# Left-side sums of the down product, begun one plain step earlier and in small tiles

## The chip, the cores and the metric

The kernel runs on one core of one Trainium2 chip. Five engines work side by side on that core: TensorE (PE in the profile, its weight loads PEld), VectorE (DVE), ScalarE (ACT), GpSimd (POOL) and SyncE (SP), which here only issues transfers. The metric is the device time of one execution in microseconds, taken as the median of three runs. The profile is of one further execution.

## The reference, cut to what matters

One decoder block on 256 tokens of width 2048, in float32: a half-step SwiGLU, a mixer (gated delta rule beside stick-breaking attention), a second half-step SwiGLU, a gated per-token embedding, and RMS norms between them. The change touches the two SwiGLU stages alone, whose inner width is 5632:

```python
def swiglu(x, w_gu, w_down):
    gate, up = jnp.split(x @ w_gu, 2, axis=-1)
    return (jax.nn.silu(gate) * up) @ w_down

h = h + 0.5 * swiglu(rms_norm(h, ffn1_norm[i]), ffn1_w_gu[i], ffn1_w_down[i])
...
h = h + 0.5 * swiglu(rms_norm(h, ffn2_norm[i]), ffn2_w_gu[i], ffn2_w_down[i])
```

## The kernel before, in words

**Numbers.** Every operand of a matmul is split into a high and a low part of the float32r type, and three matmuls (high by high, high by low, low by high) stand for one. The left side (activations, transposed) lies in `nTh`/`nTl` for the gate and up products and in `hTh`/`hTl` for the down product. One `hTh` tile holds one block of 512 inner columns as four slabs of 128 rows by 256 tokens. The weights stream in from memory: `weight_pair` (L67 to L79) loads 256 rows by 512 columns into `raw`, ScalarE casts them to `whi` (L77), VectorE subtracts to get `wlo` (L78). `whi` and `wlo` have three buffers each.

**Parts and groups.** `ffn` (L467) is called once for each SwiGLU, as "1" and "2". It walks over `PARTS` (L27): inner blocks 0 to 2, 3 to 6 and 7 to 10. Each part has one group "gu" for each of its inner blocks (gate and up, two 512-column products each for two halves of the tokens, four PSUM banks), and then two groups "dn" that multiply the part's `hTh`/`hTl` with the down weights, for output columns 0 to 1023 and 1024 to 2047. Of parts two and three, with four inner blocks each, the fourth "gu" group is called the part's last one here, and the third the one in front of it.

**Plain steps and sevenths.** In a group most rows are multiplied as they are: a plain step is 12 matmuls on one weight pair (L543 to L545), and after each `lanes.step()` (L546) lets every waiting generator go on to its next `yield`. The first `ns` row groups of 256 (`NS` = 4 for gate and up; `NS_DOWN` = 3 for down in parts two and three, 2 in part one) are instead multiplied in a seven-product scheme of 2 by 2 blocks. Its products ("sevenths", `Group.product`, L327) run inside the group before the one that they belong to: a gu group has 8 plain steps, numbered 0 to 7, and carries the seven products of its follower. `plan` (L392) puts them behind plain steps 1, 2, 3, 4, 5, 6, 7 when the follower is of the same kind, and behind 2, 3, 4, 5, 6, 7, 7 when it isn't. They run in the order of `SEVEN`: 0, 1, 2, 4, 3, 5, 6. The ones numbered 0, 4 and 6 take their left side straight from `hTh`/`hTl`, the others from sums.

**Right-side sums.** A seventh's weights come from four quarters that lie in tiles `R`. `halved` (L294) casts one to `shi` (ScalarE, L298) and subtracts to `slo` (VectorE, L299), two buffers each; `add` (L307) forms sums on VectorE, and `add_loaded` (L314) adds a quarter by a transfer of the GpSimd queue. `next_weights` (L85) writes these out ahead of the matmul that uses them: up to two further weight pairs, and one further seventh.

**Left-side sums.** `halves` (L423) makes them, in lane 1. For each two row groups it adds high and low part into a tile `S` (L455), forms four sums and differences in place (L461), casts to `Sh` (ScalarE, L463) and subtracts to `Sl` (VectorE, L464). `Sh` and `Sl` have one buffer each and are shared by the gu and the dn sums, so the dn ones can be written only when the last seventh that reads the gu ones (number 5) is done. `S` for two row groups is a tile with the tag `sil`, of one buffer, which also holds the activated gate from `gated` (L505) until `down_input` has transposed it (L485). `S` for one row group is a tile with the tag `nat`, of four buffers, which else holds the `part` copies of `product` (L349).

For the down product of parts two and three (`ns` = 3) there are thus one `S` of 1024 columns for row groups 0 and 1, and one of 512 for row group 2. The generator is added at the start of the part's last gu group (L524 to L525). It goes on behind plain step 0 (row groups 0 and 1) and, after one empty step, behind plain step 2 (row group 2).

**What sets the order.** The program is written out in this order, and a scheduler of the library then orders each engine's instructions: among those whose inputs and buffers it takes as free, the one written first. Each engine runs its own list strictly in that order on the chip. `tc.keep_in_program_order` ties an instruction behind the one written just before it on its engine. That is done for the first addition of row group 2 (L447 to L455), and for the casts and subtractions that write `hTh`/`hTl` at the end of the next group (L502, L503).

Of the kernel before, what the change touches and what calls it, by code (L numbers as in the profile page):

```python
# [10 lines left out]
F32 = mybir.dt.float32  # L11
F32R = mybir.dt.float32r
AF = mybir.ActivationFunctionType
ALU = mybir.AluOpType
# [12 lines left out]
PARTS = ((0, 3), (3, 7), (7, 11))  # L27
# [3 lines left out]
NS_DOWN = tuple(3 if i1 - i0 == 4 else 2 for i0, i1 in PARTS)  # L31


SEVEN = (0, 1, 2, 4, 3, 5, 6)
# [12 lines left out]
def block_kernel(ctx, tc, a, out):  # L47
    nc = tc.nc
# [14 lines left out]
    lanes = Lanes(4)  # L63
# [93 lines left out]
    def picker(hi, lo):  # L157
        return lambda k: (hi[k // 4][:, k % 4, :], lo[k // 4][:, k % 4, :])
# [68 lines left out]
    def block(j):  # L227
        return slice(j * NB, (j + 1) * NB)
# [191 lines left out]
    order += [("pair", a["w_pg"][2][g]) for g in range(KD // 2)] + [("pair", a["w_pp"][2])]  # L420
    order.append(("pair", a["w_pp"][3]))

    def halves(kind, his, los, ns, wait=0):  # L423


        for _ in range(wait):
            yield
        fp = current[0]

        sh = fp.tile([P, NS, 2, 2, P], F32R, tag="Sh", name="Sh")  # L430
        sl = fp.tile([P, NS, 2, 2, P], F32R, tag="Sl", name="Sl")

        def side(i, g):
            if i in (0, 4, 6):
                k, t = 2 * (g % 2) + (i > 0), i // 6
                c = slice(t * P, (t + 1) * P)
                return his[g // 2][:, k, c], los[g // 2][:, k, c]
            j, t = {1: (1, 1), 2: (0, 0), 3: (0, 1), 5: (1, 0)}[i]
            return sh[:, g, j, t, :], sl[:, g, j, t, :]

        sides[kind] = side

        for g0 in range(0, ns, 2):
            n = min(2, ns - g0)
            hi, lo = his[g0 // 2], los[g0 // 2]
            keep = lambda ins: ins
            if g0 and n == 1:  # L447

                keep = tc.keep_in_program_order
                yield  # L450
            if n == 2:
                x = fp.tile([P, 2 * NB], F32, tag="sil", name="S")
            else:
                x = act.tile([P, NB], F32, tag="nat", name="S", bufs=4)
            keep(nc.vector.tensor_tensor(out=x, in0=hi[:, 0:2 * n].bitcast(F32).rearrange("p k x -> p (k x)"),  # L455
                                         in1=lo[:, 0:2 * n].bitcast(F32).rearrange("p k x -> p (k x)"), op=ALU.add))
            xv = x.rearrange("p (g j t y) -> p g j t y", g=n, j=2, t=2)
            a11, a12, a21, a22 = (xv[:, :, j, t, :] for t in range(2) for j in range(2))
            for o, y, z, op in ((a22, a21, a22, ALU.subtract), (a21, a11, a21, ALU.subtract),
                                (a11, a22, a11, ALU.subtract), (a12, a11, a12, ALU.add)):  # L460
                nc.vector.tensor_tensor(out=o, in0=y, in1=z, op=op)  # L461
            sx = [y[:, g0:g0 + n].rearrange("p g j t y -> p (g j t y)") for y in (sh, sl)]
            nc.scalar.copy(sx[0], x)  # L463
            nc.vector.tensor_tensor(out=sx[1], in0=x, in1=sx[0], op=ALU.subtract)  # L464
            yield

    def ffn(n, nT, r, scale, next_norm, stat):  # L467
        xs = picker(*nT)
        late = callable(r)
        with tc.tile_pool(name="ffn", bufs=1) as fp:  # L470
            hTh, hTl = [], []
# [42 lines left out]
            for group, todo in ffn_plan[n]:  # L514
                if group.kind == "behind":
                    break
                dn = group.kind == "dn"
                i0 = PARTS[group.part][0]

                if dn and group.nb and not group.last:  # L520
                    lanes.add(1, halves("gu", *nT, NS))
                elif dn and group.nb and group.follower:
                    lanes.add(1, halves("behind", *nxt, NS_BEHIND, 4))
                elif not dn and group.follower.kind == "dn":  # L524
                    lanes.add(1, halves("dn", hTh[i0:], hTl[i0:], NS_DOWN[group.part]))  # L525
                if dn and group.last and nxt is None:
                    nxt = new_nT()
                if group.banks is None:
                    group.new_banks()
                for kind, one in todo:  # L530
                    if kind == "seventh":
                        group.follower.product(SEVEN[one])
                        continue
                    b, g = one
                    whi, wlo = next_weights()
                    for j in range(2):
                        k = 2 * g + j
                        xh, xl = picker(hTh, hTl)(2 * PARTS[group.part][0] * 2 + k) if dn else xs(k)
                        st, sp = not group.ns and k == 0, k == 2 * len(group.src[b]) - 1
                        for t in range(2):  # L540
                            c = slice(t * P, (t + 1) * P)
                            out = group.banks[2 * b + t]
                            nc.tensor.matmul(out, xh[:, c], whi[:, j, :], start=st, stop=False, skip_group_check=True)  # L543
                            nc.tensor.matmul(out, xh[:, c], wlo[:, j, :], start=False, stop=False, skip_group_check=True)  # L544
                            nc.tensor.matmul(out, xl[:, c], whi[:, j, :], start=False, stop=sp, skip_group_check=True)  # L545
                    lanes.step()  # L546
                    if g < len(group.src[b]) - 1:
                        continue
                    outs = group.banks[2 * b:2 * b + 2]
                    if dn:  # L550
                        nb = group.nb + b
                        for t in range(2):
                            hb = h[:, t, block(nb)]
                            nc.vector.scalar_tensor_tensor(out=hb, in0=outs[t], scalar=scale, in1=hb,
                                                           op0=ALU.mult, op1=ALU.add)
                            if group.last:
                                sumsq(stat, t, block(nb), nb)
                        if group.last:
                            norm_block(nxt, next_norm, nb, lambda: fp.tile([P, 2, 4, P], F32, tag="tT", name="tT"),
                                       mm_ps if group.follower or n == "2" else mx_ps)  # L560
                            lanes.advance(0)
                    elif b == 0:
                        if not late:
                            sil = gated(outs)
                    else:
                        if late:
                            r = r()
                            sil = gated(group.banks[0:2])
                            late = False
                        th = fp.tile([P, 4, T], F32R, tag="hTh", name="hTh", bufs=max(i1 - i0 for i0, i1 in PARTS))  # L570
                        tl = fp.tile([P, 4, T], F32R, tag="hTl", name="hTl", bufs=max(i1 - i0 for i0, i1 in PARTS))
                        hTh.append(th)
                        hTl.append(tl)
                        i0, i1 = PARTS[group.part]

                        last = (3 if i1 - i0 == 4 else 2) if len(hTh) == i1 else 0
                        gen = down_input(outs, sil, th, tl, last)
                        next(gen)

                        lanes.finish(0)  # L580
                        lanes.add(0, gen)
                        if last:
                            lanes.advance(0)
# [58 lines left out]
    with tc.tile_pool(name="fin", bufs=1) as fp:  # L642
# [34 lines left out]
        group, todo = ffn_plan["2"][-1]  # L677
        for _, (nb, g) in todo:
            whi, wlo = next_weights()
            for j in range(2):  # L680
                k = 2 * g + j
# [20 lines left out]
        for t in range(2):  # L702
            n = NB >> t
            for i in range(NB // n):
                gt = mm_ps("gt")[:, 0:n]
                products(gt, t, xs, ws, slice(i * n, (i + 1) * n))
                gated(e[t][:, i * n:(i + 1) * n], gt, slice(3 * NB + i * n, 3 * NB + (i + 1) * n), t, 3 + i)
            rt = rstd(stat, t)
            for j in range(4):
                c = slice(j * NB, (j + 1) * NB)  # L710

                if j == 0:
                    nc.scalar.activation(hf[:, t, c], hf[:, t, c], AF.Copy, scale=rt)
                else:
                    nc.vector.tensor_scalar(out=hf[:, t, c], in0=hf[:, t, c], scalar1=rt, scalar2=None, op0=ALU.mult)
                queue = nc.sync if j % 2 else nc.scalar
                queue.dma_start(out=out[t * P:(t + 1) * P, c], in_=hf[:, t, c])


class Lanes:  # L720


    def __init__(self, n):
        self.q = [[] for _ in range(n)]
# [656 lines left out]
```

## Time and profile before

| what | value |
|---|---|
| runs | 1947.93, 1948.83, 1949.49 us |
| median | 1948.83 us |
| the profiled execution's own time | 1948.68 us |
| its span, first to last instruction | 1947.0 us |
| granted TensorE clock, mean | 0.999 |
| ACT busy | 1163.5 us (60%) |
| POOL busy | 148.4 us (8%) |

The profiled execution lies 0.15 us below the median of the three runs, and 1.7 us of its time lie outside its span. Times in the profile count from the start of the span. The matmuls are pipelined: one lasts some 0.39 us by its record, and the next begins before it ends, so that PE can read as busy where it lost time. The start-to-start distance of matmuls is the better measure, and the part below uses it. The four places that the change touches are the last gu group of parts two and three in both SwiGLU stages; they begin near 340, 588, 1485 and 1733 us.

### The profile page before, as it was taken

The numbers are of one execution on the slowest core, as the hardware profiler recorded it, in microseconds if no ns is written. First come the engines' busy times: TensorE is split into PE (matmuls) and PEld (weight loads), VectorE is DVE, ScalarE is ACT, GpSimd is POOL, SyncE is SP. The second block draws the span as 40 slices with busy tenths as digits, with TensorE's granted clock in tenths as the row PEclk, the third lists the DMA queues.
The fourth block names the chain that finished last, engine by engine and source line by source line (L and its number), as shares of the span: only waits on it lengthen the run. The fifth ranks groups of instructions, "written<-read, shape, count | busy, mean of one in ns | idle before, by whom it ended". The sixth has DMA issues, their size and how long they took to land.

```text
span 1947.0 us, 24130 instructions
## 1 busy us (share of the span) xinstructions
PE 1930.5 (99%) x8884; PEld 1593.0 (82%) x8884; DVE 1569.3 (81%) x1679; ACT 1163.5 (60%) x1358; POOL 148.4 (8%) x226
## 2 busy tenths in 40 slices
PE   9999999999999999999999999999999999999998
PEld 8888888888888888878788888888888888888886
DVE  7889878997889766797856579899888987888865
ACT  7656666566565557664555456566565755656654
POOL 0011100000010000010100000010000100001000
PEclk9999999999999999999999999999999999999999
DMA  8778888788887765556565786788898987888764
GB/s 314 267 238 282 254 296 273 229 294 250 279 284 240 225 219 170 176 171 208 171 204 160 242 290 227 225 291 283 243 281 249 314 260 240 272 255 293 232 213 144
DMA packets 144182, 475.04 MB, mean 244 GB/s; under 512 B 19649, under 2 KB 47297, under 8 KB 129857
## 3 DMA queue, kind: packets, MB, share of 16 engines
q1 hardware_dynamic: 107200, 302.16, 43.9%
q0 software_dynamic: 25920, 160.44, 30.2%
q10 hardware_dynamic: 10944, 10.91, 1.8%
q8 instruction: 69, 1.13, 0.2%
q14 instruction: 49, 0.39, 0.1%
HBM read 451.44 MB, written 22.02 MB: 243 GB/s over the span
## 4 chain that ended last, share of the span: by engine, by line
PE 88%; DVE 7%; DMA 3%; ACT 1%; issue 1%; POOL 0%; SPq 0%; POOLq 0%; DVEq 0%; ACTq 0%
PE d L545 5%; PE d L543 5%; PE d L544 5%; PE g L343 4%; PE g L344 4%; PE g L342 4%; PE u L544 4%; PE u L545 4%; PE u L543 4%; PE g L544 4%; PE g L545 4%; PE pj L112 4%; PE pj L113 4%; PE pj L114 4%; PE g L543 4%; PE d L343 2%
## 5 line engine op out<-in xcount | busy, mean ns | idle before, releaser
L77 ACT CAST whi<-raw 128x1024 fp32r<-128x1024 f32 (+1 forms) x489 | 512.1, 1050 | 422.7 <-PE pj L114 99.0
L78 DVE TENSOR_TENSOR wlo<-raw,whi 128x1024 fp32r<-128x1024 f32 (+1 forms) x489 | 592.3, 1218 | 162.3 <-ACT whi L77 161.2
L299 DVE TENSOR_TENSOR slo<-R,shi 128x2048 fp32r<-128x2048 f32 (+2 forms) x224 | 444.9, 1989 | 140.0 <-ACT shi L298 138.2
L298 ACT CAST shi<-R 128x2048 fp32r<-128x2048 f32 (+2 forms) x224 | 373.5, 1671 | 128.5 <-DVE R L307 62.7
L112 PE MATMUL pj<-whi,nTh 128*128 128x512 f32 x448 | 179.4, 401 | 0.0
L113 PE MATMUL pj<-wlo,nTh 128*128 128x512 f32 x448 | 175.2, 391 | 1.1 <-DVE wlo L78 1.1
L114 PE MATMUL pj<-whi,nTl 128*128 128x512 f32 x448 | 174.9, 390 | 0.0
L543 PE MATMUL d<-whi,hTh 128*128 128x512 f32 x448 | 174.5, 390 | 0.0
L544 PE MATMUL d<-wlo,hTh 128*128 128x512 f32 x448 | 174.3, 389 | 0.0
L545 PE MATMUL d<-whi,hTl 128*128 128x512 f32 x448 | 173.4, 389 | 0.0
L544 PE MATMUL g<-wlo,nTh 128*128 128x512 f32 x400 | 156.0, 390 | 0.5 <-DVE wlo L78 0.5
L544 PE MATMUL u<-wlo,nTh 128*128 128x512 f32 x400 | 155.7, 389 | 0.4 <-DVE wlo L78 0.4
L545 PE MATMUL g<-whi,nTl 128*128 128x512 f32 x400 | 155.8, 389 | 0.0
L545 PE MATMUL u<-whi,nTl 128*128 128x512 f32 x400 | 155.7, 389 | 0.0
L543 PE MATMUL g<-whi,nTh 128*128 128x512 f32 x400 | 155.3, 390 | 0.0
L543 PE MATMUL u<-whi,nTh 128*128 128x512 f32 x400 | 154.1, 389 | 0.0
L307 DVE TENSOR_TENSOR R<-R 128x2048 f32<-128x2048 f32 (+2 forms) x68 | 135.8, 1996 | 0.1
L113 PEld LDWEIGHTS pj<-wlo,nTh 128*128 128x128 f32 x448 | 84.2, 188 | 18.9 <-DVE wlo L78 2.6
L543 PEld LDWEIGHTS d<-whi,hTh 128*128 128x128 f32 x448 | 84.1, 188 | 18.2 <-ACT hTh L502 1.0
L545 PEld LDWEIGHTS d<-whi,hTl 128*128 128x128 f32 x448 | 84.1, 188 | 17.8
L114 PEld LDWEIGHTS pj<-whi,nTl 128*128 128x128 f32 x448 | 84.1, 188 | 17.5
L544 PEld LDWEIGHTS d<-wlo,hTh 128*128 128x128 f32 x448 | 84.1, 188 | 17.4
(332 smaller groups left out, 3444.1 us busy)
## 6 DMA issues: line engine op xcount, KB each, us to landing
raw<-in_w_gu SPq DMA_DIRECT2D x199, 512.0 KB, 5.7
raw<-in_w_down SPq DMA_DIRECT2D x112, 512.0 KB, 6.9
raw<-in_w_in SPq DMA_DIRECT2D x112, 512.0 KB, 3.4
R<-in_w_gu2q POOLq DMA_DIRECT2D x54, 1024.0 KB, 8.6
R<-in_w_gu1q POOLq DMA_DIRECT2D x48, 1024.0 KB, 8.6
raw<-in_w_out SPq DMA_DIRECT2D x32, 512.0 KB, 4.5
tT<-scr SPq DMA_DIRECT2D x22, 512.0 KB, 5.0
R<-in_w_down11q POOLq DMA_DIRECT2D x12, 768.0 KB, 6.2
```

What stands on the lines that cost most here:

```text
L77: nc.scalar.copy(hi[:, j, :], raw[:, j, :])
L78: nc.vector.tensor_tensor(out=lo[:, j, :], in0=raw[:, j, :], in1=hi[:, j, :], op=ALU.subtract)
L112: nc.tensor.matmul(outs[t], xh[:, c], whi[:, j, :], start=st, stop=False)
L113: nc.tensor.matmul(outs[t], xh[:, c], wlo[:, j, :], start=False, stop=False)
L114: nc.tensor.matmul(outs[t], xl[:, c], whi[:, j, :], start=False, stop=sp)
L298: keep(nc.scalar.copy(hi, w))
L299: nc.vector.tensor_tensor(out=lo, in0=w, in1=hi, op=ALU.subtract)
L307: keep(nc.vector.tensor_tensor(out=self.raw[x], in0=self.raw[x], in1=self.raw[y], op=ALU.add))
L343: nc.tensor.matmul(out, xh, wlo[:, g, :], start=False, stop=False, skip_group_check=True)
L543: nc.tensor.matmul(out, xh[:, c], whi[:, j, :], start=st, stop=False, skip_group_check=True)
L544: nc.tensor.matmul(out, xh[:, c], wlo[:, j, :], start=False, stop=False, skip_group_check=True)
L545: nc.tensor.matmul(out, xl[:, c], whi[:, j, :], start=False, stop=sp, skip_group_check=True)
```

## The change

For parts two and three the generator of the down sums is no longer added at the start of the part's last gu group. It is added in the group in front of it, right behind seventh number 5 of that group's follower, the last that reads the gu sums. It goes on first behind plain step 7 of that group, then twice in the last group, behind plain steps 0 (empty) and 1. So each of its pieces is written one plain step sooner. It also goes through the row groups one at a time (`at_once` = 1): three `S` tiles of 512 columns, all of the tag `nat`, in place of one of 1024 of the tag `sil` and one of 512. Row groups 0 and 1 are still written in one go, and row group 2 keeps its tie to the instruction written before it. `Later` looks the `hTh` tiles up when they are used, since the last ones don't exist yet when the generator is made. Part one, the gu sums and the ones called "behind" stay as they are.

```diff
-    def halves(kind, his, los, ns, wait=0):
+    def halves(kind, his, los, ns, wait=0, at_once=2):
...
-        for g0 in range(0, ns, 2):
-            n = min(2, ns - g0)
-            hi, lo = his[g0 // 2], los[g0 // 2]
+        for g0 in range(0, ns, at_once):
+            n = min(at_once, ns - g0)
+            k0 = 2 * (g0 % 2)
+            hi, lo = (x[g0 // 2][:, k0:k0 + 2 * n] for x in (his, los))
             keep = lambda ins: ins
-            if g0 and n == 1:
+            if g0 == 2 and n == 1:
...
-            yield
+            if not g0 % 2 + n == 1 or g0 + n == ns:
+                yield
...
-                elif not dn and group.follower.kind == "dn":
+                elif not dn and group.follower.kind == "dn" and not group.part:
                     lanes.add(1, halves("dn", hTh[i0:], hTl[i0:], NS_DOWN[group.part]))
...
                     if kind == "seventh":
-                        group.follower.product(SEVEN[one])
+                        follower = group.follower
+                        follower.product(SEVEN[one])
+                        if group.part and not dn and one == 5 and follower.kind == "gu" and \
+                                follower.follower.kind == "dn":
+                            p = PARTS[group.part][0]
+                            lanes.add(1, halves("dn", Later(hTh, p), Later(hTl, p), NS_DOWN[group.part], 0, 1))
                         continue
...
+class Later:
+
+
+    def __init__(self, blocks, first):
+        self.blocks, self.first = blocks, first
+
+    def __getitem__(self, i):
+        return self.blocks[self.first + i]
```

More of the change, by code (lines that the diff above doesn't have):

```diff
@@ L454, in halves @@
                 x = act.tile([P, NB], F32, tag="nat", name="S", bufs=4)
-            keep(nc.vector.tensor_tensor(out=x, in0=hi[:, 0:2 * n].bitcast(F32).rearrange("p k x -> p (k x)"),
-                                         in1=lo[:, 0:2 * n].bitcast(F32).rearrange("p k x -> p (k x)"), op=ALU.add))
+            keep(nc.vector.tensor_tensor(out=x, in0=hi.bitcast(F32).rearrange("p k x -> p (k x)"),
+                                         in1=lo.bitcast(F32).rearrange("p k x -> p (k x)"), op=ALU.add))
             xv = x.rearrange("p (g j t y) -> p g j t y", g=n, j=2, t=2)
```

## The prediction

> **What bounds the kernel now.** I read the page first, then the busy time by stretches, and last the timelines of single engines round the four places of the change.
>
> ```profile
> span 1947.0 us, 24130 instructions
> ...
> PE 1930.5 (99%) x8884; PEld 1593.0 (82%) x8884; DVE 1569.3 (81%) x1679; ACT 1163.5 (60%) x1358; POOL 148.4 (8%) x226
> ```
>
> PE is busy 99% of the span and the matmuls aren't changed, so the most that can be won is the time in which PE starts its matmuls late. A stretch without trouble and the four places of the change, by stretches of 48 us (columns: us, then for each engine busy us and instructions):
>
> ```profile
> 230.00:278.00 48.00, 48.00 (x214) 39.73 (x213) 37.32 (x26) 29.20 (x26) 4.84 (x7) 1.00 0.86 267
> ...
> 340.00:388.00 48.00, 47.64 (x209) 38.41 (x208) 43.24 (x46) 27.96 (x30) 4.84 (x7) 1.00 0.77 227
> 588.00:636.00 48.00, 47.64 (x208) 38.41 (x207) 43.23 (x45) 28.27 (x30) 4.84 (x7) 1.00 0.77 227
> 1485.00:1533.00 48.00, 47.64 (x208) 38.43 (x207) 43.23 (x45) 28.36 (x30) 4.80 (x7) 1.00 0.77 229
> 1733.00:1781.00 48.00, 47.64 (x208) 38.43 (x207) 43.23 (x45) 28.69 (x30) 4.79 (x7) 1.00 0.78 227
> ```
>
> The reader is to see the second column: 214 matmuls in the clean stretch, 208 or 209 in the others. The granted clock (1.00) is the same, so 5 or 6 matmuls' time is lost at each place. The four rows are alike, so I work out the first and multiply by four. Its PE timeline has the size:
>
> ```profile
> 340.08 0.39 PE L543 MATMUL g<-whi,nTh 128*128 128x512 f32 x1
> ...
> 348.01 0.39 PE L545 MATMUL g<-whi,nTl 128*128 128x512 f32 x1
> 348.24 0.39 PE L342 MATMUL d<-shi,hTh 128*128 128x512 f32 x1
> ...
> 362.98 0.50 PE L342 MATMUL d<-shi,Sh 128*128 128x512 f32 x1
> 363.32 0.40 PE L343 MATMUL d<-slo,Sh 128*128 128x512 f32 x1
> ...
> 368.20 0.40 PE L545 MATMUL u<-whi,nTl 128*128 128x512 f32 x1
> 368.73 0.50 PE L343 MATMUL d<-slo,hTh 128*128 128x512 f32 x1
> 369.07 0.40 PE L344 MATMUL d<-shi,hTl 128*128 128x512 f32 x1
> ...
> 376.57 0.39 PE L342 MATMUL d<-shi,hTh 128*128 128x512 f32 x1
> 377.18 0.50 PE L343 MATMUL d<-slo,hTh 128*128 128x512 f32 x1 [0.22 <-DVE slo L299]
> 377.52 0.40 PE L344 MATMUL d<-shi,hTl 128*128 128x512 f32 x1
> ```
>
> From 340.08 to 348.01 lie the 36 matmuls of three plain steps, 35 distances: 7.93 / 35 = 0.227 us each. The five long distances are 0.34, 0.53, 0.34, 0.61 and 0.34 us, together 2.16; less 5 x 0.227 = 1.13 they lose **1.03 us**. Smaller ones of some 0.01 us between them add the rest: by the counts, (214 - 209) x 0.227 = 1.1 to (214 - 208) x 0.227 = 1.4 us. I take 1.03 as the sure part and 1.2 as all of it, so 4.1 to 4.8 us for the four places.
>
> Why PE waits there is in the timelines of DVE and then of ACT for the same place, and in the busy time of the three stretches before, in and behind the crowd (third engine column: DVE):
>
> ```profile
> 301.71 1.28 DVE L503 TENSOR_TENSOR hTl<-tT,hTh 128x512 fp32r<-128x512 f32 x2
> ...
> 336.36 1.76 DVE L299 TENSOR_TENSOR slo<-R,shi 128x1536 fp32r<-128x1536 f32 x1 [1.10 <-ACT shi L298]
> ...
> 343.35 1.30 DVE L485 STREAM_TRANSPOSE tb<-sil 128x512 f32<-128x512 f32 x2
> ...
> 345.68 1.22 DVE L455 TENSOR_TENSOR S<-hTh,hTl 128x1024 f32<-128x1024 f32 x1
> ...
> 351.74 1.22 DVE L78 TENSOR_TENSOR wlo<-raw,whi 128x1024 fp32r<-128x1024 f32 x1
> ...
> 354.09 0.69 DVE L455 TENSOR_TENSOR S<-hTh,hTl 128x512 f32<-128x512 f32 x1
> 354.84 1.76 DVE L299 TENSOR_TENSOR slo<-R,shi 128x1536 fp32r<-128x1536 f32 x1
> ...
> 363.59 0.68 DVE L464 TENSOR_TENSOR Sl<-S,Sh 128x512 fp32r<-128x512 f32 x1
> 366.92 1.76 DVE L299 TENSOR_TENSOR slo<-R,shi 128x1536 fp32r<-128x1536 f32 x1 [2.65 <-ACT shi L298]
> ```
> ```profile
> 333.07 1.14 ACT L502 CAST hTh<-tT 128x512 fp32r<-128x512 f32 x2
> 334.84 1.49 ACT L298 CAST shi<-R 128x1536 fp32r<-128x1536 f32 x1 [0.63 <-PE u L344]
> ...
> 365.40 1.48 ACT L298 CAST shi<-R 128x1536 fp32r<-128x1536 f32 x1
> ```
> ```profile
> 303.00:336.40 33.40, 33.40 (x149) 27.67 (x148) 27.46 (x20) 22.28 (x22) 3.07 (x5) 1.00 0.94 278
> 336.40:360.80 24.40, 24.40 (x109) 20.19 (x109) 24.26 (x28) 11.49 (x12) 1.77 (x2) 1.00 0.73 205
> 360.80:382.00 21.20, 20.84 (x90) 16.25 (x89) 16.57 (x18) 14.31 (x15) 2.19 (x4) 1.00 0.83 294
> ```
>
> DVE is full from 336.4 to 360.8 (24.26 of 24.40 us), has 5.9 us to spare in the 33.4 us before, and 4.6 us to spare right after, where PE then waits for DVE. So the trouble is order. Row group 2 starts at 354.09 and its `Sl` ends at 364.27, ten microseconds for six short DVE instructions and one cast, as other work lies between them. Sevenths 1 and 2 can't end before that, so both `shi`/`slo` buffers stay taken, the next `shi` cast waits until 365.40 and the next `slo` until 366.92. From there the subtractions follow each other too closely, and PE catches up with one at 368.20 and with another at 376.57.
>
> **The change part by part.** First the durations, from the rows of the tile `S` in that place (min/median/max ns; the smaller is the short form):
>
> ```profile
> L461 DVE TENSOR_TENSOR S<-S x8: 282/353/424, 348.5 to 360.5; 128x256 f32<-128x256 f32 x4, 128x128 f32<-128x128 f32 x4
> L455 DVE TENSOR_TENSOR S<-hTh,hTl x2: 687/952/1218, 345.7 to 354.1; 128x1024 f32<-128x1024 f32 x1, 128x512 f32<-128x512 f32 x1
> L463 ACT CAST Sh<-S x2: 619/838/1057, 351.9 to 362.3; 128x1024 fp32r<-128x1024 f32 x1, 128x512 fp32r<-128x512 f32 x1
> L464 DVE TENSOR_TENSOR Sl<-S,Sh x2: 684/954/1225, 352.9 to 363.6; 128x1024 fp32r<-128x1024 f32 x1, 128x512 fp32r<-128x512 f32 x1
> ```
>
> *Tiles.* Row groups 0 and 1 cost now 1.22 + 4 x 0.42 + 1.23 = 4.1 us on DVE and 1.06 on ACT. As two small tiles they cost 2 x (0.69 + 4 x 0.28 + 0.68) = 5.0 us on DVE and 1.24 on ACT: **0.9 us more DVE** and 0.2 us more ACT at each place. Hidden, it costs nothing; with DVE full and nothing given back, 4 x 0.9 = 3.5 us.
>
> [...]
>
> *Start.* Now the large `S` waits for its `sil` buffer until the transposes have read it (343.35 + 1.30), so it could not begin sooner however early it was written; it begins at 345.68. A `nat` buffer is free long before. That sums of this kind run ahead of the place where they are written shows the next pair of rows: the gu sums of the following group begin at 391.30, while the evictions of the group in front, written before them, run at 412.95 and later.
>
> ```profile
> 391.30 1.23 DVE L455 TENSOR_TENSOR S<-nTh,nTl 128x1024 f32<-128x1024 f32 x1
> ...
> 412.95 1.28 DVE L554 SCALAR_TENSOR_TENSOR h<-d,h 128x512 f32<-128x512 f32 x2
> ```
>
> Row groups 0 and 1 read only the part's first block, whose last piece is finished at 302.99 (301.71 + 1.28). So I expect their additions, 2 x (0.69 + 4 x 0.28) = 3.6 us, in the 5.9 us to spare between 303 and 336.4, at no cost. Their `Sh` and `Sl` must wait for seventh 5 of the gu group, as `Sh` is shared; PE ends it near 334.8, since the `shi` cast of 334.84 waits for the same seventh. They then fall into the DVE hole of 1.10 us that ends at 336.36.
>
> *The crowd.* The DVE work between 336.4 and 360.8 loses 4.1 us and gets at most 1.4 us (two `Sl`) back. Of it, 2.9 us (1.22 + 4 x 0.42) lie ahead of the `wlo` of 351.74. Row group 2 moves from behind that `wlo` to ahead of it, 0.69 + 4 x 0.28 = 1.8 us. It so starts some 5 us sooner, near 349, and ends by about 354 in place of 364.27, as seventh 1 needs it (PE reaches it 9 + 12 matmuls behind 348.24, at 348.24 + 21 x 0.227 = 353.0). The `slo` that now runs at 366.92 then follows seventh 1 as soon as its buffer is free, near 356: the 4.6 us that DVE has to spare behind 360.8 are used before it. Of PE's waits 0.53 and 0.61 us, with the 0.34 us behind each and the 0.34 at 362.98, none has a cause left.
>
> *Moved past.* ACT's casts of `hTh` for the block in front are tied behind the new `Sh` casts. Behind them wait the next `shi` and `whi`, and DVE's `hTl`: with two small casts (1.24 us) and the two of `hTh` (1.14 us) ahead of it, the `shi` of 334.84 slips by up to 2.4 us, and its `slo` from 336.36 to 338.8, done at 340.5. The seventh that needs them starts at 348.24, so over 7 us cover it. If that cover were gone, 2.4 us would show at each place. SP and POOL get no new transfer; POOL's adding transfers wait only on R and its readers. The extra `nat` tiles hold three of four buffers at most, while the `part` copies use one at a time. I find nothing in these rows that is late next, but a first use of a fresh operand costs 0.34 - 0.227 = 0.1 us, as the three distances of 0.34 show, and one may stay.
>
> *Sum.* Four places x 1.05 us (between the sure 1.03 and 1.2 less 0.1) = **4.2 us**. The profiled execution's 1948.68 would become 1944.5; it lies 0.15 us below the median of the runs shown, so I predict 1948.83 - 4.2 = **1944.6 us**. All of it gone is 1944.0.
>
> **The rivals.**
>
> *Half of it.* The wait at 368.20 goes, but the order that the scheduler now finds leaves the one at 376.57, or makes a like one, as the list of each engine is fixed and PE's lead over `slo` is small there. For it: this second wait comes eight microseconds after the first, with other sevenths. Against: it is the same backlog. That leaves some 0.6 us of 1.2, so 4 x 0.55 = 2.2 us gained: 1946.6 us.
>
> *It doesn't do what it says.* Row group 2, which ends last, is still drawn out by the work between its instructions. Then sevenths 1 and 2 end as late as now: 1948.8 us.
>
> *The crowd moves forward (slower).* If the small tiles of row groups 0 and 1 do not run ahead, they are done where they are written, from 335.3 on: 5.0 us, less the hole of 1.10, push everything by 3.9 us. The `wlo` of 351.74 then comes at 351.74 + 3.9 - 2.9 + 1.8 = 354.5 and ends at 355.8, while PE first uses it at 353.90:
>
> ```profile
> 353.90 0.39 PE L544 MATMUL u<-wlo,nTh 128*128 128x512 f32 x1
> ```
>
> PE would wait 1.9 us and lose 0.1 more at the next start: 2.0 us at each place. It decides from the point where that `wlo` ends over 0.94 us later than now (351.74 + 1.22 = 352.96). With the old waits gone the net is +0.8 x 4 (1952.1 us), with all of them still there +2.0 x 4 (1956.8); I take the middle, 1954.4 us. Against it is the row of 391.30.
>
> *Only the price is paid.* DVE stays the limit through the whole crowd, nothing is gained, and the 0.9 us show: + 3.5 us, 1952.3 us. [...] Against it: DVE has 5.9 us free before and 4.6 us behind.
>
> **How the numbers follow.** Full effect 0.52, half 0.27, no effect 0.08, crowd forward 0.09, only the price 0.04. A measurement of this kernel can tell about 0.2% from no change, that is 3.9 us. The full effect reaches from 3.4 to 4.8 us; I give 0.46 to more than 3.9 and 0.06 to less. Faster is then 0.46. Within 0.2% lie 0.06 + 0.27 + 0.08, the price's 0.04 and 0.02 of the crowd: 0.47. Slower is 0.07. The range has to hold the full and the half effect (0.79): from 1944.0, less 0.5 for the spread of the runs, 1943.5, up to 1948.3, half a microsecond short of no effect, since the waits that remain in the half case may be 1.1 us each. The likeliest case's own range is 1943.5 to 1945.6.
>
> **What would show it.** Right: matmul counts of 212 to 214 in the four stretches; no distance over 0.3 us between the sevenths of the down group; `S` of row groups 0 and 1 before 336 us, and the `Sl` of row group 2 by about 355; DVE with nothing left idle at 361 to 367. Wrong: `S` of 512 columns only from 335 on, with a wait on `wlo` near 354 (crowd forward); `Sl` of row group 2 after 360 (no effect); a `slo` wait of 0.3 us or more near 376 (half). The prediction is wrong as a whole if the scheduler's new order costs PE time away from these four places, which I haven't priced because no row of the trace points to a place.

## The result and the profile after

The changed kernel takes **1958.34 us** (median of six runs, 1958.13 to 1959.99) against 1948.91 us for the kernel before (six runs, 1947.93 to 1949.49). The ratio is 1.0051, with an interval of 1.004 to 1.0061: some 9.4 us slower, where 4.2 us less were predicted. The profiled execution took 1958.19 us.

First the page of the changed kernel, span and busy times:

```profile
span 1956.5 us, 24152 instructions
...
PE 1933.3 (99%) x8884; PEld 1594.1 (81%) x8884; DVE 1573.7 (80%) x1703; ACT 1163.2 (59%) x1362; POOL 148.4 (8%) x226
```

The work on the engines is nearly what it was: DVE has 4.4 us more over the whole kernel (1573.7 less 1569.3). That isn't the price of the small tiles: the kernel below that has them at the old place keeps DVE busy for 1569.9 us. PE has the same 8884 matmuls. So the loss is again in late starts. Here are the busy times of the clean stretch and of the four places, by the same stretches as before (us, then for each engine busy us and instructions; then the granted clock):

```profile
230.00:278.00 48.00, 48.00 (x214) 39.74 (x213) 37.15 (x26) 29.18 (x25) 4.85 (x7) 1.00 0.87 267
340.00:388.00 48.00, 45.54 (x198) 36.44 (x197) 41.94 (x43) 27.40 (x31) 4.84 (x7) 1.00 0.75 225
588.00:636.00 48.00, 46.21 (x201) 37.20 (x200) 42.46 (x51) 27.16 (x31) 4.19 (x7) 1.00 0.74 239
1485.00:1533.00 48.00, 45.28 (x190) 36.14 (x189) 41.30 (x51) 27.06 (x30) 3.96 (x7) 0.96 0.75 238
1733.00:1781.00 48.00, 46.93 (x204) 37.84 (x203) 43.20 (x51) 28.88 (x32) 4.44 (x7) 1.00 0.79 257
```

The reader is to see the matmuls: 198, 201, 190 and 204 in place of 209, 208, 208 and 208. That is 11 + 7 + 18 + 4 = 40 fewer, and 40 x 0.227 us = 9.1 us, nearly all of the 9.5 us between the two profiled executions. The clean stretch has its 214 as before. The old five distances at each place gave way to longer ones, as the PE timeline at the first place shows:

```profile
349.14 0.39 PE L342 MATMUL d<-shi,hTh 128*128 128x512 f32 x1
...
358.66 0.39 PE L342 MATMUL d<-shi,Sh 128*128 128x512 f32 x1
359.42 0.74 PE L550 MATMUL u<-whi,nTh 128*128 128x512 f32 x2 [0.38 <-ACT whi L77]
360.27 0.51 PE L343 MATMUL d<-slo,Sh 128*128 128x512 f32 x1
360.62 0.40 PE L344 MATMUL d<-shi,Sl 128*128 128x512 f32 x1
...
375.83 0.39 PE L344 MATMUL d<-shi,Sl 128*128 128x512 f32 x1
376.89 0.50 PE L342 MATMUL d<-shi,hTh 128*128 128x512 f32 x1 [0.68 <-ACT shi L298]
378.69 0.50 PE L343 MATMUL d<-slo,hTh 128*128 128x512 f32 x1 [1.29 <-DVE slo L299]
379.03 0.40 PE L344 MATMUL d<-shi,hTl 128*128 128x512 f32 x1
```

The first row is for comparison. This matmul, the first of the sevenths for the down group, starts at 349.14 here and at 348.24 in the kernel before. The same 0.9 us lies between the two ahead of all that the change moves (DVE's last subtraction of a `part` copy before it, 330.92 and 330.02), so 0.9 us of any difference in time between these two traces is no effect of the change.

There are two groups of waits: from 358.66 to 360.62 lie four distances (two matmuls share the row of 359.42), 1.96 - 4 x 0.227 = 1.05 us lost, waiting for a weight cast `whi` and a `slo`; from 375.83 to 379.03 three distances, 3.20 - 0.68 = 2.5 us lost, waiting for `shi` and `slo`. The next two views show what DVE and then ACT did (the changed lines shift the numbers by one or two: the sums' additions are L456 and L462, `Sh` L464, `Sl` L465). The `slo` for which PE waits at 360.27 is the one of 358.46:

```profile
336.07 1.29 DVE L456 TENSOR_TENSOR S<-hTh,hTl 128x512 f32<-128x512 f32 x2
337.27 1.70 DVE L462 TENSOR_TENSOR S<-S 128x128 f32<-128x128 f32 x8
...
340.06 1.29 DVE L465 TENSOR_TENSOR Sl<-S,Sh 128x512 fp32r<-128x512 f32 x2 [0.42 <-ACT Sh L464]
...
344.26 1.76 DVE L299 TENSOR_TENSOR slo<-R,shi 128x1536 fp32r<-128x1536 f32 x1
...
351.59 1.22 DVE L78 TENSOR_TENSOR wlo<-raw,whi 128x1024 fp32r<-128x1024 f32 x1
352.72 1.75 DVE L307 TENSOR_TENSOR R<-R 128x1536 f32<-128x1536 f32 x1
354.39 0.69 DVE L456 TENSOR_TENSOR S<-hTh,hTl 128x512 f32<-128x512 f32 x1
...
358.46 1.76 DVE L299 TENSOR_TENSOR slo<-R,shi 128x1536 fp32r<-128x1536 f32 x1 [0.69 <-ACT shi L298]
```
```profile
356.42 0.62 ACT L464 CAST Sh<-S 128x512 fp32r<-128x512 f32 x1 [4.48 <-DVE S L462]
356.95 1.48 ACT L298 CAST shi<-R 128x1536 fp32r<-128x1536 f32 x1
358.32 1.04 ACT L77 CAST whi<-raw 128x1024 fp32r<-128x1024 f32 x1
...
372.90 1.05 ACT L77 CAST whi<-raw 128x1024 fp32r<-128x1024 f32 x1 [4.38 <-DMA raw<-in_w_down]
```

Row groups 0 and 1 were added at 336.07 and not in the spare time before 336. Row group 2 began at 354.39 in place of 354.09; counted from PE's first seventh that is 0.6 us sooner and not five. And ACT stood idle for 4.48 us, until 356.42, in front of row group 2's `Sh` cast, with a `shi` and a `whi` behind it in its list. In the kernel before the same `shi` and `whi` stood ahead of that cast, which came at 362.31 there:

```profile
353.33 1.48 ACT L298 CAST shi<-R 128x1536 fp32r<-128x1536 f32 x1
354.71 1.05 ACT L77 CAST whi<-raw 128x1024 fp32r<-128x1024 f32 x1
```

They slipped by 3.6 us each, 2.7 us when counted from PE's first seventh, the `whi` up to the moment when PE waits for it. Fifteen microseconds on, ACT waits 4.38 us for a weight load, and PE for the casts behind it.

### The profile page after: what moved, and what is told of

Read it like the earlier page. It is cut to its first block, busy times and chain, and to the rows that moved or that the text cites. A ratio compares the mean times of both kernels' runs of the same rounds, so it can differ in the third digit from the quotient of the medians.

```text
span 1956.5 us, 24152 instructions
## 1 busy us (share of the span) xinstructions
PE 1933.3 (99%) x8884; PEld 1594.1 (81%) x8884; DVE 1573.7 (80%) x1703; ACT 1163.2 (59%) x1362; POOL 148.4 (8%) x226
## 4 chain that ended last, share of the span: by engine, by line
PE 84%; DVE 7%; DMA 5%; issue 2%; ACT 1%; ACTq 0%; POOL 0%; SPq 0%; DVEq 0%; POOLq 0%
PE d L550 5%; PE d L551 5%; PE d L552 5%; PE g L342 4%; PE g L343 4%; PE g L344 4%; PE pj L112 4%; PE pj L113 4%; PE pj L114 4%; PE u L551 4%; PE u L552 4%; PE u L550 4%; PE g L551 3%; PE g L552 3%; PE g L550 3%; DVE wlo L78 2%
```

## The experiments

All kernels below compute the whole result; medians and ratios are against the kernel before, in runs on the same chip. The first four ask which part of the change costs: the place where the sums are begun (the expectations say PLACE), the small tiles (TILES), or a `tT` transfer that now stands ahead of weight loads in SP's queue (QUEUE).

**Small tiles at the old place.** The new `lanes.add` is taken out and the old one serves all parts, with `at_once` = 1 for parts two and three.

```diff
-                elif not dn and group.follower.kind == "dn" and not group.part:
-                    lanes.add(1, halves("dn", hTh[i0:], hTl[i0:], NS_DOWN[group.part]))
+                elif not dn and group.follower.kind == "dn":
+                    lanes.add(1, halves("dn", hTh[i0:], hTl[i0:], NS_DOWN[group.part], 0, 1 if group.part else 2))
...
-                        if group.part and not dn and one == 5 and follower.kind == "gu" and \
-                                follower.follower.kind == "dn":
+                        if False:
```

> Small tiles alone: the three tiles of 512 columns, but written at the old place (behind plain steps 0 and 2 of the part's last group). Theory PLACE (the loss comes from the five microseconds of VectorE work for row groups 0 and 1 now standing in front of the group's first weight splits and right-side sums): no loss, 1945 to 1950 us. Theory TILES (the loss comes from the small tiles, 0.9 us more VectorE work at each place): 1952 us or more. Theory QUEUE (the transposed block's read tT comes late on the SP queue and the weight loads behind it): tT issued near 353 us as before, so 1945 to 1950 us as well.

Measured: 1945.21 us (ten runs, 1944.31 to 1946.36), ratio 0.9982 [0.9973, 0.9992], 3.4 us faster than before. That is in the range of PLACE and of QUEUE and rules out TILES. The small tiles aren't the cost; at the old place they win most of what there is to win. Matmuls in the four stretches: 212, 213, 212, 213.

**The `tT` transfer later.** In the change, the transfer that reads the transposed block back is written two yields later for the part's last block but one.

```diff
-                for _ in range(2 if last else 4):
+                late_tT = not last and len(hTh) == i1 - 1 and i1 > 3
+                for _ in range(2 if last else 6 if late_tT else 4):
...
-                for _ in range(last or 6):
+                for _ in range(last or (4 if late_tT else 6)):
```

> The change, but in the part's last group the read tT of the block in front is written two plain steps later, so that weight loads go ahead of it on the SP queue. Theory QUEUE: the loads of the down weights no longer wait behind tT near 361 us, the PE waits of 0.8 and 1.6 us near 376 shrink below 0.5 us at all four places, 1950 to 1954 us. Theory PLACE without the queue: the waits stay, 1957 to 1960 us. Theory TILES: 1957 to 1960 us.

Measured: 1954.31 us (eight runs, 1953.01 to 1954.78), ratio 1.0027 [1.0017, 1.0037]. It gives back 4 of the 9.4 us, a little less than QUEUE had expected. Of the waits near 376 the one for `shi` goes, but the one for `slo` stays at 1.29 us. ACT still has the long wait of 4.48 us for row group 2's `Sh` cast, which starts at 356.86. The queue is a part of the later waits, and not their origin.

**Another buffer for row group 0.** In the change, the first `S` tile takes a tag of its own in place of `nat`, so that it needn't wait for a buffer.

```diff
-                x = act.tile([P, NB], F32, tag="nat", name="S", bufs=4)
+                x = act.tile([P, NB], F32, tag="junk", name="S", bufs=1) if kind == "dn" and g0 == 0 else \
+                    act.tile([P, NB], F32, tag="nat", name="S", bufs=4)
```

> The change, but the tile S of row group 0 lies in the buffer of the tag junk, which nothing else uses at that time; the one of row group 1 stays in nat. If the tiles failed to run ahead because a nat buffer is handed out in written order, behind the part copies of the same group: row group 0 is done near 314 to 330 us, row group 1 still near 336. Theory PLACE: with half of the five microseconds gone from the crowd about half of the loss goes, 1951 to 1955 us. Theories TILES and QUEUE (if the lateness of tT has another cause): 1957 to 1960 us.

Measured: 1944.86 us (ten runs, 1943.86 to 1946.05), ratio 0.9981 [0.9972, 0.999]. The DVE timeline shows the two row groups apart, and the ACT timeline the cast of row group 2:

```profile
314.70 0.69 DVE L457 TENSOR_TENSOR S<-hTh,hTl 128x512 f32<-128x512 f32 x1
...
336.46 0.68 DVE L457 TENSOR_TENSOR S<-hTh,hTl 128x512 f32<-128x512 f32 x1
```
```profile
354.74 0.62 ACT L465 CAST Sh<-S 128x512 fp32r<-128x512 f32 x1 [7.24 <-DVE S L463]
...
357.16 1.04 ACT L77 CAST whi<-raw 128x1024 fp32r<-128x1024 f32 x1
```

The time is below all that the three theories had for this kernel. Row group 0, with its own buffer, runs ahead by 21 us, as was predicted for both; row group 1, still in `nat`, does not. So it is the buffer that held them. ACT waits for row group 2's cast here too, for 7.24 us, but it comes 1.7 us sooner than in the change.

**Row group 2 back at its old step.** In the change, one more `yield` ahead of row group 2.

```diff
                 keep = tc.keep_in_program_order
                 yield
+                if at_once == 1:
+                    yield
```

> The change, but row group 2 is written behind plain step 2 of the last group as before; row groups 0 and 1 stay one step sooner. If the sooner place of row group 2 (ahead of the weight split of plain step 4 and of the right side of seventh 2) makes the PE waits of 0.5 and 0.3 us near 358.7: these go, 1953 to 1956 us. Theory PLACE (row groups 0 and 1 are what matters): the waits near 376 stay, 1956 to 1961 us.

Measured: 1958.28 us (four runs, 1956.12 to 1959.44), ratio 1.0047 [1.0032, 1.0062]: as slow as the change, as PLACE had it. ACT again waits 4.48 us for that cast. What row group 2's additions are written behind is not what costs.

The next three ask whether the early additions in DVE's list are the price (HOLE), or something that is written sooner (SOONER).

**One seventh later.** The sums are added behind seventh number 6 of the follower, and advanced once there.

```diff
-                        if group.part and not dn and one == 5 and follower.kind == "gu" and \
+                        if group.part and not dn and one == 6 and follower.kind == "gu" and \
                                 follower.follower.kind == "dn":
                             p = PARTS[group.part][0]
                             lanes.add(1, halves("dn", Later(hTh, p), Later(hTl, p), NS_DOWN[group.part], 0, 1))
+                            lanes.advance(1)
```

> The change, but row groups 0 and 1 are written behind seventh 6 of the group in front, half a step later: the right side of the last group's first seventh (its slo and the sum R behind it) is then written first and goes first. Row group 2 stays at the change's place. Theory HOLE (what hurts is that the sums take the VectorE hole near 336 us, in which that slo ran before, and push it and R by five to eight microseconds): slo again near 336 to 338, R near 341 to 343, no PE wait over 0.4 us, 1944 to 1947 us. Theory SOONER (any start ahead of plain step 0 crowds VectorE, whatever goes first): 1952 us or more.

Measured: 1944.10 us (ten runs, 1943.00 to 1944.95), ratio 0.9975 [0.9966, 0.9985], with 213 matmuls in all four stretches. This is what HOLE had expected, and SOONER is out: `slo` runs at 337.11 and `R` at 342.44. But a second thing differs from the change. Its row group 2 is no sooner than the change's (its `S` begins at 354.38), but on ACT the next `shi` goes ahead of its cast:

```profile
354.56 1.48 ACT L298 CAST shi<-R 128x1536 fp32r<-128x1536 f32 x1 [2.76 <-DVE R L307]
356.41 0.62 ACT L464 CAST Sh<-S 128x512 fp32r<-128x512 f32 x1 [0.37 <-DVE S L462]
```

**Made-up work.** The kernel before, with four additions of 128x512 into `nat` tiles that nobody reads, at the place where the change writes its sums.

```diff
+                    if group.part and not dn and group.follower.kind == "gu" and group.follower.follower.kind == "dn" \
+                            and (b, g) == group.plain[-1]:
+                        for _ in range(4):
+                            made_up = act.tile([P, NB], F32, tag="nat", name="made_up", bufs=4)
+                            nc.vector.tensor_tensor(out=made_up, in0=hTh[i0][:, 0:2].bitcast(F32).rearrange("p k x -> p (k x)"),
+                                                    in1=hTl[i0][:, 0:2].bitcast(F32).rearrange("p k x -> p (k x)"), op=ALU.add)
```

> The kernel before, with four additions of 128 by 512 into a spare buffer (2.5 us of VectorE work that nothing uses) written at the place where the change writes the sums; all else as before. Theory HOLE: work of any kind at this place pushes slo and R of the first seventh, and the time goes up by several microseconds though the sums themselves stand where they stood: 1952 to 1960 us. If instead the loss comes from the sums' own casts, buffers or ties: 1948 to 1951 us.

Measured: 1950.42 us (ten runs, 1949.80 to 1951.27), ratio 1.0009 [1.0, 1.0018]. DVE work of 2.5 us pushed into that place costs 1.8 us in all (206, 205, 206 and 206 matmuls). That is outside HOLE's range, and inside the one for a loss from the sums' own casts, buffers or ties. It delays the `slo` of 336.36 to 341.10 only, where the change has 344.26; the kernel with the late cast, below, delays it as far as the change does.

**Own buffers, old place and new.** Two kernels in which row groups 0 and 1 take tags of their own (`nat` keeps three buffers): the first at the old place, the second at the change's.

```diff
...
-                x = act.tile([P, NB], F32, tag="nat", name="S", bufs=4)
+                tag, bufs = {0: ("junk", 1), 1: ("own", 1), 2: ("nat", 3)}[g0]
+                x = act.tile([P, NB], F32, tag=tag, name="S", bufs=bufs)
...
```

> Small tiles written at the old place, with a buffer of their own for each of row groups 0 and 1 (the tag nat gives one up for it). Both then run ahead, near 314 to 330 us, in free time of VectorE. If free time there costs nothing: 1943.5 to 1945 us, as in the prediction. If running ahead delays work there: above the 1945.2 us of the small tiles at the old place in nat.

> The change as it stands (casts and row group 2 one step sooner), with a buffer of their own for each of row groups 0 and 1. The additions run ahead as the prediction had it. If the prediction failed only in this step: 1943.5 to 1945.6 us, its likeliest case. If the sooner place of the casts (ahead of the hTh casts and the next shi on ScalarE) or of row group 2 costs something too: 1947 us or more.

Measured: 1945.41 us (ten runs, 1944.06 to 1946.45), ratio 0.9982 [0.9973, 0.9992], at the old place; 1944.95 us (nine runs, 1943.02 to 1945.74; a tenth took 9126.6 us and isn't counted), ratio 0.998 [0.997, 0.9989], at the new one. The first is 0.2 us above the small tiles in `nat` at the old place, well inside the spread of the runs, so that it does not matter there whether the additions run ahead. The second is in the likeliest range of the prediction. In it, DVE and ACT do what the prediction had said:

```profile
314.93 1.29 DVE L457 TENSOR_TENSOR S<-hTh,hTl 128x512 f32<-128x512 f32 x2
...
350.50 0.69 DVE L457 TENSOR_TENSOR S<-hTh,hTl 128x512 f32<-128x512 f32 x1
```
```profile
352.53 0.62 ACT L465 CAST Sh<-S 128x512 fp32r<-128x512 f32 x1 [5.56 <-DVE S L463]
353.06 1.05 ACT L77 CAST whi<-raw 128x1024 fp32r<-128x1024 f32 x1
...
354.53 1.48 ACT L298 CAST shi<-R 128x1536 fp32r<-128x1536 f32 x1
```

Note ACT: it waits 5.56 us for row group 2's cast, longer than in the change, with the same two casts behind it, and hardly anything is lost (213 or 214 matmuls in the four stretches). The length of the wait isn't the price; the moment at which it ends is what differs.

The last two test that moment: is it the place of one cast in ACT's list (CAST), or the transfers that come late with the rest (TRANSFERS)?

**The cast later.** In the change, two yields ahead of row group 2's `Sh` cast, and so of its `Sl` too, which is written right behind the cast.

```diff
             sx = [y[:, g0:g0 + n].rearrange("p g j t y -> p (g j t y)") for y in (sh, sl)]
+            if at_once == 1 and g0 == 2:
+                yield
+                yield
             nc.scalar.copy(sx[0], x)
```

> The change, but the cast Sh of row group 2 is written two plain steps behind its sums, so that on ScalarE the shi of seventh 2 and the next whi go ahead of it. Theory CAST (ScalarE stands 4.5 us for that cast, since the sums of row group 2 are late on VectorE, and what is behind it, shi, whi and through whi the freeing of the raw buffers and the next weight loads, is late by as much): the waits near 358.7 and those near 376 both shrink, weight loads from 358 on, 1945 to 1950 us. Theory TRANSFERS (the adding transfer of GpSimd comes four microseconds late and meets the block's write and read on the DMA engines): only the waits near 358.7 go, 1953 to 1956 us.

Measured: **1943.75 us** (nine runs, 1942.52 to 1944.71), ratio 0.9975 [0.9964, 0.9985], the fastest of all, 1.3 us below what CAST had expected and far from TRANSFERS. Its DVE timeline has the `slo` and row group 2 as late as in the change, so the early additions aren't the price by themselves:

```profile
344.46 1.75 DVE L299 TENSOR_TENSOR slo<-R,shi 128x1536 fp32r<-128x1536 f32 x1
...
354.59 0.69 DVE L456 TENSOR_TENSOR S<-hTh,hTl 128x512 f32<-128x512 f32 x1
```

On ACT, two casts go ahead of the late one:

```profile
354.77 1.49 ACT L298 CAST shi<-R 128x1536 fp32r<-128x1536 f32 x1 [2.62 <-DVE R L307]
356.16 1.05 ACT L77 CAST whi<-raw 128x1024 fp32r<-128x1024 f32 x1
357.10 0.62 ACT L467 CAST Sh<-S 128x512 fp32r<-128x512 f32 x1
...
369.05 1.05 ACT L77 CAST whi<-raw 128x1024 fp32r<-128x1024 f32 x1
```

and by the busy times of the four places PE starts 213, 213, 214 and 213 matmuls, of 214 in the clean stretch (the first row):

```profile
340.00:388.00 48.00, 48.00 (x213) 39.75 (x213) 45.85 (x45) 29.07 (x33) 4.84 (x7) 1.00 0.81 239
```

The later waits vanish with the earlier ones, though the `tT` transfer is as late as in the change. The fifth `whi` from there on is cast at 369.05, with no wait for its load, and not at 372.90. Its load is issued at the same time in both (behind the `tT` transfer of 361.56 here, of 361.32 in the change), so it was some 4 us longer under way in the change. Beside it there were the `tT` transfer, in both kernels, and an `R` transfer that GpSimd issues at 360.52 in the change and at 358.56 here, as it waits for a `slo`. From 345 to 380 the median load of `raw` takes 9.6 us from issue to landing in the change and 8.2 us here, the `tT` transfer 8.2 and 6.1 us. That the other two got in the load's way is my reading of these times; which of them delays which was not tried, other than by the later `tT`, which gave back 4 us.

**One `shi` tied behind the cast.** The kernel of seventh 6, with the next `shi` tied behind row group 2's cast.

```diff
...
-                keep(nc.scalar.copy(hi, w))
+                cast = keep(nc.scalar.copy(hi, w))
+                if third:
+                    tc.add_manual_dep(cast.ins, third.pop().ins.name, mybir.DependencyInfo(
+                        mybir.DependencyClass.NoSync, mybir.DependencyReason.DATA), reason="behind")
...
-            nc.scalar.copy(sx[0], x)
+            cast = nc.scalar.copy(sx[0], x)
+            if at_once == 1 and g0 == 2:
+                third.append(cast)
...
```

> The kernel with the sums behind seventh 6 (1944.1 us), but the shi of seventh 2 is tied behind the cast of row group 2 on ScalarE, as the scheduler had put it in the change; the next whi stays ahead. Theory CAST: shi and slo of seventh 2 come 1.9 us later, PE waits of about 1 us near 358 at all four places, 1947 to 1950 us; with whi in time the weight loads are not late and the waits near 376 stay away. Theory TRANSFERS: no waits, 1944 to 1945.5 us.

Measured: 1945.48 us (ten runs, 1944.15 to 1946.27), ratio 0.9983 [0.9974, 0.9993], 1.4 us above the kernel without the tie (their intervals overlap). That is in the range of TRANSFERS and not in CAST's, which had counted on a late `shi` alone to cost 3 to 6 us. The ACT timeline:

```profile
351.93 1.05 ACT L77 CAST whi<-raw 128x1024 fp32r<-128x1024 f32 x1
...
356.64 0.62 ACT L467 CAST Sh<-S 128x512 fp32r<-128x512 f32 x1 [2.46 <-DVE S L465]
357.17 1.48 ACT L298 CAST shi<-R 128x1536 fp32r<-128x1536 f32 x1
```

Cast and `shi` run as late as in the change, 0.2 us later even, but the `whi` had gone ahead, at 351.93. So a `shi` as late as the change's costs little by itself. That the late `whi` is the greater part fits PE's first wait, which is for it, but isn't shown: no kernel has the late `whi` alone, and this one differs from the change also in its row groups 0 and 1 and in its `tT` transfer (355.41 and not 361.32).

## Why the prediction was wrong

*What bounds the kernel* was right. The lost starts at the four places were 1.03 to 1.2 us each; the kernel with the late cast loses next to none of them and is 4.7 us faster than before (1948.44 in its runs), against 4.1 to 4.8 us for all of it. The number itself, 1944.6, is close to what the change gives with own buffers (1944.95). One detail was misread: the 0.34 us are not the price of the first use of an operand. They stand behind late starts; the first use of the `shi` of 348.24 is followed by the next matmul at 348.46.

*Tiles* was sized too high, without harm, as the sum took it as hidden. It added up the durations of single instructions, which overlap where they follow each other (eight of 0.288 us take 1.70 us in the change, not 2.30). By the merged rows row groups 0 and 1 take 1.29 + 1.70 + 1.29 = 4.3 us on DVE in the change, and 1.22 + 0.42 + 1.34 + 1.23 = 4.2 us before (rows of 345.68, 348.48, 350.48 and 352.95): 0.1 us more at each place and not 0.9. With small tiles at the old place DVE is busy for 0.6 us more in the whole kernel. So the 3.5 us of *Only the price is paid* had no such price behind them.

*Start* is the step that failed first. "A `nat` buffer is free long before" was taken from the number of buffers and not from a row. With a tag of its own, row group 0 ran at 314.70; without one, row group 1 ran at 336.46. In `nat` the first addition starts at 335.23, 336.07 and 335.92 when it is written at the old place, at the change's and behind seventh 6; less the 0.05, 0.90 and 0.75 us by which PE's first seventh is later in these traces than the 348.24 of before, this is 335.2 in all three. So the tag set this time, and the place of writing did not. That the `part` copies written ahead of the sums held the buffer is the likely reason; no run shows it by itself. The row of 391.30 that was to show that sums run ahead is of a large `S`, in tag `sil`; it says nothing of `nat`. So the additions came at 336.07, ahead of the `slo` that went from 336.36 to 344.26.

*The crowd* fell with it. Row group 2 was to start near 349; it started at 354.39, behind the `slo`, `wlo` and `R` of 344 to 354, which the early sums had pushed. With own buffers it starts at 350.50.

*Moved past* is the step that set the sign. It counted what waits behind the casts of `hTh`, found nothing that is late next, and so put this term at nothing. It didn't look at the last of the moved casts, row group 2's `Sh`. Written sooner, it stands in ACT's list ahead of a `shi` and a `whi`, and ACT takes its list in order: it idled 4.48 us, though the `shi` had its `R` from 352.72 + 1.75 = 354.47 on, and the `whi` could have gone at 351.93, as the kernel with the tied `shi` shows. With the cast over by 353.15 (own buffers for both) or even by 355.36 (for row group 0; `Sh` at 354.74, `whi` at 357.16), little or nothing is lost; at 356.42, with `whi` at 358.32, PE waits and loses 1.05 us. The 1.16 us between those two `whi` casts (0.84 us when counted from PE's first seventh, 348.82 and 349.14) is about that loss, so my estimate is that the slack is used up near the earlier of the two. So neither half costs by itself: late sums with the cast behind (1943.75) are fast, an early place in the list with sums in time (1944.95) is fast, and both together cost 9.4 us. Moving the one cast, with its `Sl`, takes all of it away. The way from the cast to the first waits is in the rows above; the way to the later ones, by the transfers, is only read from the traces, and a part of the price is the granted clock of 0.51 shown at the end.

None of the rivals had the time. *The rival of the crowd that moves forward* came nearest, with 1954.4. It had the right premise: small tiles that don't run ahead, from 335.3 on, where 336.07 came. Its place and price were not right, and that it comes near is luck: the `wlo` of 351.74 came at 351.59, PE did not wait for it, and the kernel with the late cast has the same early sums and loses nothing by them. (Its lower end, 1948.83 + 3.2, is 1952.0 and not 1952.1.) The reason given against it, the row of 391.30, was the same error as in *Start*.

## What to carry to other kernels

When work is written sooner, follow every instruction of it to the list of its own engine: a cast that gets ahead of others must also have its input ahead of theirs, or they wait with it (here ACT idled 4.48 us in front of one, with a `shi` and a `whi` behind it). A claim that a buffer is free needs a row that shows an instruction take one of that tag out of turn. A small wait that is hidden stays hidden only up to a point; find which consumer sets that point (here most likely a weight cast with about a microsecond of slack) before the wait is priced at nothing or at its length.

## What the runs showed of the hardware

At the third place the change loses 18 matmuls and not 11. Here are its PE timeline there, the busy time of the stretches round it, and last that of the like stretch at the first place:

```profile
1526.36 0.50 PE L342 MATMUL d<-shi,hTh 128*128 128x512 f32 x1 [0.95 <-ACT shi L298]
1528.15 0.80 PE L343 MATMUL d<-slo,hTh 128*128 128x512 f32 x1 [1.29 <-DVE slo L299]
1528.75 0.63 PE L344 MATMUL d<-shi,hTl 128*128 128x512 f32 x1
...
1530.88 0.63 PE L343 MATMUL d<-slo,hTh 128*128 128x512 f32 x1
```
```profile
1525.00:1528.70 3.70, 1.46 (x4) 0.69 (x3) 3.03 (x4) 3.62 (x3) 0.31 (x1) 0.91 1.02 422
1528.70:1531.50 2.80, 2.80 (x8) 2.18 (x7) 2.80 (x5) 0.00 (x0) 0.22 (x1) 0.51 0.87 278
...
375.00:378.70 3.70, 1.73 (x8) 0.88 (x6) 2.73 (x4) 3.70 (x4) 0.00 (x0) 1.00 1.02 420
```

Behind the two waits the matmuls start 0.426 us apart ((1530.88 - 1528.75) / 5) and not 0.227, at a granted clock of 0.51, for 2.8 us; that adds at least 5 x 0.2 = 1.0 us at this place. At the first place the same two waits are followed by the full clock (1.00 from 379 to 382, with 0.23 us from start to start). With the later `tT` transfer all four stretches have the full clock (1.00, where the third has 0.96 in the change), so by my estimate some 1 us of the 4 us gained there is this. At the third place the trace shows no single idle time longer than 1.29 us, but 3.7 us in which PE was busy for 1.46; the first place, with 1.73 of 3.70, kept its clock. The kernel with row group 2 back at its old step shows that no bound between these two figures sets it. There the first place falls to a granted clock of 0.55 over 3.7 us, behind a stretch that was busier:

```profile
375.00:378.70 3.70, 2.07 (x9) 1.18 (x8) 2.73 (x4) 3.70 (x4) 0.00 (x0) 1.00 1.03 425
378.70:382.40 3.70, 3.70 (x10) 2.92 (x11) 3.70 (x5) 0.36 (x1) 0.54 (x1) 0.55 1.00 355
```

So PE's busy time in such a stretch doesn't decide by itself whether the clock falls: it stayed at 1.00 behind 1.73 of 3.70 us and fell to 0.55 behind 2.07. What else does stays open.
